# A hybrid diffusion step on one core: modulation vectors on 32-column quarters of the array, and four key heads projected before the vectors' second half

## The chip, the core and the metric

The kernel runs on one core of a Trainium2 chip. It is one launch; the metric is its device time in microseconds. Before the change three runs took 2576.31, 2579.31 and 2580.29 us, median 2579.31.

## What is computed

One layer of a hybrid backbone over 128 context tokens and 2048 latent tokens of 1024 features: modulated RMS norm, a combined projection into gated DeltaNet heads and gated spatial MLP groups, output projection, modulated norm, a squared-ReLU MLP, and a last norm. The change touches only the opening: the modulation vectors and the first projection.

```python
def modulation(cond, w_mod_l, b_mod_l):
    m = jax.nn.silu(cond) @ w_mod_l + b_mod_l
    return jnp.split(m[:, None, :], N_MOD, axis=-1)

def block(x, s0, mod, ...):
    sh1, sc1, ga1, sh2, sc2, ga2 = mod
    h = rmsnorm(x, norm_mix_l) * (1.0 + sc1) + sh1
    o, s_new = mixer(h, s0, ...)
    ...

def mixer(h, ...):
    proj = h @ w_in_l
    ...
    qkv = jax.nn.silu(centred_conv(qkv, conv_l))
```

There are two condition vectors, one for the context and one for the latent tokens (`c_ctx`, `c`), so each modulation product is a 2 x 1024 matrix times a 1024-column part of `w_mod`. All is float32.

## The kernel before

The 17 tiles of 128 tokens go through the first stage in six blocks of up to three tiles (`BLOCKS`). Features lie on partitions, as eight pieces k = 0 to 7 of 128 (`KT`). A projection is three fp32r products per k (`mm3`, L220 to L222): high part times high part, low times high, high times low; each operand is split into a high and a low part by ACT and DVE (`split_w`: ACT casts `raw` to `wH`, L191, DVE subtracts for `wL`, L192).

The opening goes as follows. `scond` (128 x 8 x 2) holds the activated condition vectors. A modulation vector is computed in halves of 512 columns: the scale `a1` and the shift `b1` of the first norm have four such halves, m0 (first half of b1), m1 (first half of a1), m2 and m3 (second halves of b1 and a1). `mod_load` fetches one as eight pieces of 256 KB. `mod_columns` makes eight fp32 products that add into two rows of one PSUM bank (L335, stationary `scond[:, k, :]`, 2 columns), copies them to SBUF on ACT (L337), and turns the 2 x 512 row into columns by four transposes (L340); DVE adds the bias and forms the scale (L343, L347).

The first half of the vectors serves k = 0 to 3, the second half k = 4 to 7. `column(k)` in `prep_block` makes the modulated features of one k for the first block: three transposes of the normalised token tiles (L482), two evictions on ACT with scale and shift (`full`, L484), then cast and subtraction on DVE (`kH`, L487, and `kL`, L488). `feature_tile` projects one head of one kind (`gi` 0 queries, 1 keys, 2 values); its `main` steps are the eight k. `first_half` shifts the halo columns, which POOL copies into `kH` and `kL`. `norm_rows` squares a token tile on ACT (L318), takes the root on POOL (L178) and scales on DVE (L320). The three token tiles and the 10 halo rows `xh` share three buffers, so the third tile takes the buffer of `xh` once that has been transposed (L387). `make_masks` builds masks on POOL from a DVE memset (L129, L135, L137) and DVE combines them (L141). Beside the block's projections run the alpha/beta projection (`ab_block`, L609, L610) and one more modulation vector (`split_mod_steps`, L359, L360).

All loads and stores are issued by SyncE, in one order; eight are in flight at a time, and the next is issued when the eighth before it has landed. The order on each engine is not the program's text: the build schedules the instructions, and what stands in the built program decides. Each engine then works through its own list and waits at semaphores.

Of the kernel before, what the change touches and what calls it, by code (L numbers as in the profile page):

```python
# [8 lines left out]
F32 = mybir.dt.float32  # L9
# [5 lines left out]
ALU = mybir.AluOpType  # L15
# [47 lines left out]
def hybrid_step(  # L63
# [217 lines left out]
    with ExitStack() as ph:  # L281
# [27 lines left out]
        V.scalar_tensor_tensor(out=st_, in0=st_, scalar=1.0, in1=cvec, op0=ALU.add, op1=ALU.mult)  # L309
        V.tensor_scalar_mul(scond.rearrange("p k c -> p c k"), st_.rearrange("p (c k) -> p c k", c=2), 0.5)  # L310

        def norm_rows(dst):

            np_ = dst.shape[0]
            junk = p1.tile([P, D], BF16, tag="junk", name="junk", bufs=1)
            ss = smp.tile([P, 1], F32, tag="ss", name="ss")
            r = smp.tile([P, 1], F32, tag="r", name="r")
            A.activation(junk[:np_, :], dst, AF.Square, accum_out=ss[:np_, :])  # L318
            rsqrt_cols(r[:np_, :], ss[:np_, :], 1, 1.0 / D, EPS)
            V.tensor_scalar_mul(dst, dst, r[:np_, :])  # L320
# [7 lines left out]
            return [raw_w(w_mod[0, k * P : (k + 1) * P, c0 + half * 512 : c0 + half * 512 + 512])  # L328
                    for k in range(KT)]

        def mod_columns(raws, half, dst, bias, scaled):

            pm = pm1()
            for k in range(KT):
                T.matmul(pm[0:2, :], scond[:, k, :], raws[k], start=k == 0, stop=k == KT - 1)  # L335
            row = p1.tile([2, 512], F32, tag="mrow", name="mrow", bufs=1)
            A.copy(row, pm[0:2, :])  # L337
            pc = pm1()
            for i in range(4):
                T.transpose(pc[:, 2 * i : 2 * i + 2], row[:, i * P : (i + 1) * P], ident[0:2, 0:2])  # L340
            ks = slice(half * 4, half * 4 + 4)
            d = dst[:, :, ks]
            V.tensor_tensor(out=d, in0=pc[:, 0:8].rearrange("p (k c) -> p c k", c=2),  # L343
                            in1=bias[:, ks].unsqueeze(1).to_broadcast([P, 2, 4]), op=ALU.add)
            if scaled:
                for cd in range(2):
                    V.scalar_tensor_tensor(out=dst[:, cd, ks], in0=dst[:, cd, ks], scalar=1.0,  # L347
                                           in1=vec[:, 16 + half * 4 : 20 + half * 4], op0=ALU.add, op1=ALU.mult)
# [22 lines left out]
        load(out=vec, in_=v_columns)  # L371
        convw = vec[:, 32:68].rearrange("p (w a) -> p w a", w=3)
        m1 = mod_load(0, D)
        mod_columns(m0, 0, b1, vec[:, 0:8], False)


        xh = p1.tile([P, D], F32, tag="x", name="xh", bufs=3)[0:10, :]
# [19 lines left out]
        def load_w1(gi, ks):  # L397
            return [w1_raw(gi, k) for k in ks]
# [329 lines left out]
        blk, xs_, cols = prep_block(0)  # L728
        for st in xs_:
            st()  # L730
        m2 = mod_load(1, 0)
        m3 = mod_load(1, D)
        wr = load_w1(1, range(4))
        mod_columns(m1, 0, a1, vec[:, 8:16], True)
        W1[1] += [split_w(r) for r in wr]
        first_half(0)
        abr = p1.tile([P, KT, 16], F32, tag="abr", name="abr", bufs=1)
        load(out=abr, in_=w_ab)
        wk = load_w1(1, range(4, KT))
        wr = load_w1(0, range(KT))  # L740
        us = [feature_tile(blk, 0, 1, h) for h in range(3)]
        for k in range(4):
            cols[k]()
            for u in us:
                u["main"][k]()
        mod_columns(m2, 1, b1, vec[:, 0:8], False)
        mod_columns(m3, 1, a1, vec[:, 8:16], True)
        W1[1] += [split_w(r) for r in wk]
        first_half(1)
        for k in range(4, KT):  # L750
# [9 lines left out]
        for bi in range(len(BLOCKS)):  # L760
            nxt = prep_block(bi + 1) if bi + 1 < len(BLOCKS) else None
            if bi == 0:
                order = [(1, 0), (1, 1), (1, 2), (0, 0), (0, 1), (1, 3), (0, 2), (0, 3)]
            else:
                order = [(gi, h) for gi in (1, 0) for h in range(4)]
            order = order + [(2, h) for h in range(4)]
            at = {e: n for n, e in enumerate(order)}
            tile_of = {}
            for n, (gi, h) in enumerate(order):
                u = us[n] if bi == 0 and n < 3 else feature_tile(blk, bi, gi, h)  # L770
                tile_of[gi, h] = u
                main = u["main"][4:] if bi == 0 and n < 3 else u["main"]
                if bi == 0 and n < 2:
                    side += wq[4 * n : 4 * n + 4]
                if bi == 0 and 2 <= n <= 5:
# [1334 lines left out]
```

## Time and profile before

| what | us |
|---|---|
| median of three runs | 2579.31 |
| span of the profiled execution, first to last instruction | 2574.7 |
| TensorE busy in it | 2542.1 (99%) |
| VectorE, ScalarE, GpSimd busy | 1781.9, 1192.5, 313.9 |
| first projection (first L220) begins | 41.30 |

The page gives the profiled execution's span; no separate time for that execution is listed, and the span lies 4.6 us below the median of the runs. Reading the rows: PE is TensorE's matmul stream, PEld its weight loads, DVE VectorE, ACT ScalarE, POOL GpSimd, SPq the issuing of transfers by SyncE. A row of the timeline has the start in us, the length, the engine, the line, the operation, what it writes and reads, its shape and count, and in brackets the idle time ahead of it with what ended it. An fp32 product shows as two passes, so eight products read x16. A row of a stretch has the busy time and number of instructions of PE, PEld, DVE, ACT and POOL, then the granted TensorE clock (1.00 is full), the busy share of the transfer engines and GB/s.

### The profile page before, as it was taken

How to read it: one execution, taken by the hardware profiler on the slowest of the kernel's cores; microseconds unless marked ns; L12 is line 12 of the kernel's file. 1: busy time of each engine (PE TensorE's matmuls, PEld its weight loads, DVE VectorE, ACT ScalarE, POOL GpSimd, SP SyncE). 2: the span in 40 equal slices, each digit the busy share in tenths (PEclk: the TensorE clock that was granted, in tenths of full speed). 3: DMA queues.
4: the chain of work that ended last, by engine and by line, in shares of the span. 5: the costliest groups of instructions: out<-in, count | busy, mean ns of one | idle time of the engine just before them, and what ended most of it. 6: DMA issues, size and time to landing. Idle time of an engine off the chain costs nothing.

```text
span 2574.7 us, 43713 instructions
## 1 busy us (share of the span) xinstructions
PE 2542.1 (99%) x15296; PEld 2134.4 (83%) x15296; DVE 1781.9 (69%) x3524; ACT 1192.5 (46%) x2758; POOL 313.9 (12%) x512
## 2 busy tenths in 40 slices
PE   8999999999999999999999999999999999999998
PEld 4999999788888778888888888888888888888887
DVE  5777746666667788885587887677674445675874
ACT  4755555554545556763355553333243333243441
POOL 3112112222222233331000000000000000000000
PEclk9999999999999999999999999999999999999999
DMA  8966637755555758896778798445599878786773
GB/s 293 297 221 208 197 118 231 235 165 168 165 168 177 229 185 261 280 311 209 268 219 252 214 292 284 140 144 155 177 298 310 279 261 301 238 258 212 232 251 107
DMA packets 533859, 579.77 MB, mean 225 GB/s; under 512 B 35500, under 2 KB 366684, under 8 KB 530054
## 3 DMA queue, kind: packets, MB, share of 16 engines
q1 hardware_dynamic: 533638, 576.98, 70.5%
q8 instruction: 120, 1.97, 0.3%
q14 instruction: 101, 0.83, 0.1%
HBM read 397.62 MB, written 179.22 MB: 224 GB/s over the span
## 4 chain that ended last, share of the span: by engine, by line
PE 55%; DVE 1%; issue 1%; DMA 0%; ACT 0%; POOL 0%; SPq 0%; DVEq 0%; POOLq 0%; ACTq 0%
PE f L220 17%; PE f L221 17%; PE f L222 17%; PE pj L220 1%; PE pj L222 1%; PE pj L221 1%; PE f L856 0%; PE pd L992 0%; PE pd L1096 0%; PE pd L1097 0%; DMA gr<-g_d 0%; PE pm L1418 0%; DMA x<-in_x_sample_dram 0%; PE pd L1060 0%; PE f L270 0%
## 5 line engine op out<-in xcount | busy, mean ns | idle before, releaser
L220 PE MATMUL f<-hop,zH 128*128 128x512 f32 x960 | 373.2, 389 | 0.0
L222 PE MATMUL f<-hop,zL 128*128 128x512 f32 x960 | 373.1, 389 | 0.0
L221 PE MATMUL f<-hop,zH 128*128 128x512 f32 x960 | 373.1, 389 | 0.0
L220 PE MATMUL f<-hop,wH 128*128 128x512 f32 x896 | 351.5, 393 | 0.0
L221 PE MATMUL f<-hop,wH 128*128 128x512 f32 x896 | 348.9, 390 | 0.0
L222 PE MATMUL f<-hop,wL 128*128 128x512 f32 x896 | 344.3, 390 | 0.0
L1604 ACT CAST zH<-zraw 128x512 fp32r<-128x512 f32 x240 | 146.5, 620 | 296.0 <-DMA zraw<-s_d 92.7
L1598 DVE TENSOR_TENSOR zL<-zraw,zH 128x512 fp32r<-128x512 f32 x240 | 162.1, 687 | 72.7 <-ACT zH L1604 61.6
L220 PEld LDWEIGHTS f<-hop,zH 128*128 128x128 f32 x960 | 180.3, 188 | 37.3
L222 PEld LDWEIGHTS f<-hop,zL 128*128 128x128 f32 x960 | 180.2, 188 | 37.3
L221 PEld LDWEIGHTS f<-hop,zH 128*128 128x128 f32 x960 | 180.2, 188 | 37.3
L222 PEld LDWEIGHTS f<-hop,wL 128*128 128x128 f32 x896 | 168.2, 188 | 35.6
L220 PEld LDWEIGHTS f<-hop,wH 128*128 128x128 f32 x896 | 168.5, 188 | 34.1 <-issue 0.9
L221 PEld LDWEIGHTS f<-hop,wH 128*128 128x128 f32 x896 | 168.6, 188 | 32.2
L222 PE MATMUL pj<-kH,wL 128*128 128x386 f32 (+2 forms) x568 | 190.6, 335 | 0.0
L220 PE MATMUL pj<-kH,wH 128*128 128x386 f32 (+2 forms) x568 | 189.1, 336 | 0.3 <-DVE kH L487 0.3
L221 PE MATMUL pj<-kL,wH 128*128 128x386 f32 (+2 forms) x568 | 189.3, 333 | 0.0
L178 POOL TENSOR_TENSOR r<-rsq,nhalf 128x1 f32<-128x1 f32 (+1 forms) x38 | 22.3, 587 | 1352.4 <-DVE rsq L177 1352.4
L1751 ACT CAST wH<-s 128x512 fp32r<-128x512 f32 x96 | 58.9, 620 | 172.8 <-DVE s L1598 157.3
L537 DVE SCALAR_TENSOR_TENSOR cv<-pj,vec,cv 128x384 f32<-128x384 f32 (+2 forms) x164 | 87.1, 538 | 58.4 <-ACT cv L534 57.0
L220 PEld LDWEIGHTS pj<-kH,wH 128*128 128x128 f32 x568 | 107.1, 189 | 4.9 <-issue 4.4
L221 PEld LDWEIGHTS pj<-kL,wH 128*128 128x128 f32 x568 | 107.4, 189 | 0.6
(408 smaller groups left out, 5729.3 us busy)
## 6 DMA issues: line engine op xcount, KB each, us to landing
zraw<-z_d SPq DMA_DIRECT2D x212, 256.0 KB
raw<-in_w_ff_dram SPq DMA_DIRECT2D x128, 256.0 KB
hop<-hop_d SPq DMA_DIRECT2D x28, 1024.0 KB
z_d<-c SPq DMA_DIRECT2D x96, 256.0 KB
zraw<-s_d SPq DMA_DIRECT2D x96, 256.0 KB
raw<-in_w_mod_dram SPq DMA_DIRECT2D x80, 256.0 KB
r<-in_w_ff_dram SPq DMA_DIRECT2D x80, 256.0 KB
s_d<-s SPq DMA_DIRECT2D x64, 256.0 KB
```

The source lines that it names most:

```text
L178: G.tensor_tensor(out=out, in0=t[:np_, :n], in1=nhalf[:np_, :n], op=ALU.pow)
L220: T.matmul(ps, lh, rh, start=first and i == 0, stop=False, skip_group_check=more)
L221: T.matmul(ps, lh, rl, start=False, stop=False, skip_group_check=more)
L222: T.matmul(ps, ll, rh, start=False, stop=last and i == n - 1, skip_group_check=more)
L537: V.scalar_tensor_tensor(out=cv[:, o : o + m], in0=ps[:, s + sh : s + sh + m], scalar=convw[:, w, j : j + 1], in1=cv[:, o : o + m], op0=AL ...
L1598: V.tensor_tensor(out=out, in0=a, in1=b, op=op)
L1604: A.copy(h, src)
L1751: A.copy(h, s2)
```

## The change

`scond` is laid out again as `sc32`, 32 columns per k of which two are filled and 30 are zero. `mod_products` replaces the loop of L335: product k goes to the 32 columns of the array (and the 32 PSUM partitions) at 32 * (k % 4), so four partial sums of two products each form in the four quarters. `mod_columns` copies all 128 rows and, in place of the four transposes, multiplies by `sel`, a 128 x 2 matrix with ones that picks and adds the four quarters. The first four key weight pieces are loaded ahead of m2 and m3. Four key heads (before: three) are projected over k = 0 to 3, and between these steps the products of m2 and m3 are placed, four at a time; `in_row` fixes their order on TensorE. The list of heads of block 0 has the fourth key head ahead of the first query head.

```diff
+        sc32 = p1.tile([P, KT, 32], F32, tag="sc32", name="sc32", bufs=1)
+        V.memset(sc32, 0.0)
+        V.tensor_copy(sc32[:, :, 0:2], scond)
+        sel = smp.tile([P, 2], F32, tag="sel", name="sel", bufs=1)
+        V.tensor_copy(sel, ident[:, 0:2])
+        for j in range(1, 4):
+            V.tensor_tensor(out=sel, in0=sel, in1=ident[:, 32 * j : 32 * j + 2], op=ALU.add)
+
+        row_end = []
+
+        def in_row(fn):
+
+            start = len(tc.nc.cur_bb.bb.instructions)
+            fn()
+            made = [x for x in tc.nc.cur_bb.bb.instructions[start:] if x.engine == mybir.EngineType.PE]
+            for x in made:
+                if row_end:
+                    tc.add_manual_dep(x, row_end[-1].name, mybir.DependencyInfo(
+                        mybir.DependencyClass.NoSync, mybir.DependencyReason.DATA), reason="order")
+            row_end.append(made[-1])
...
-        def mod_columns(raws, half, dst, bias, scaled):
+        def mod_products(raws):
 
             pm = pm1()
-            for k in range(KT):
-                T.matmul(pm[0:2, :], scond[:, k, :], raws[k], start=k == 0, stop=k == KT - 1)
-            row = p1.tile([2, 512], F32, tag="mrow", name="mrow", bufs=1)
-            A.copy(row, pm[0:2, :])
+
+            def part(k0, k1):
+                for k in range(k0, k1):
+                    j = 32 * (k % 4)
+                    T.matmul(pm[j : j + 32, :], sc32[:, k, :], raws[k], start=k < 4, stop=k >= 4)
+
+            return pm, part
+
+        def mod_columns(pm, half, dst, bias, scaled):
+
+            row = p1.tile([P, 512], F32, tag="mrow", name="mrow", bufs=1)
+            A.copy(row, pm)
             pc = pm1()
             for i in range(4):
-                T.transpose(pc[:, 2 * i : 2 * i + 2], row[:, i * P : (i + 1) * P], ident[0:2, 0:2])
+                T.matmul(pc[:, 2 * i : 2 * i + 2], row[:, i * P : (i + 1) * P], sel, start=True, stop=True)
...
-        mod_columns(m0, 0, b1, vec[:, 0:8], False)
+        pm, part = mod_products(m0)
+        part(0, KT)
+        mod_columns(pm, 0, b1, vec[:, 0:8], False)
...
+        wr = load_w1(1, range(4))
         m2 = mod_load(1, 0)
         m3 = mod_load(1, D)
-        wr = load_w1(1, range(4))
-        mod_columns(m1, 0, a1, vec[:, 8:16], True)
+        pm, part = mod_products(m1)
+        part(0, KT)
+        mod_columns(pm, 0, a1, vec[:, 8:16], True)
...
-        us = [feature_tile(blk, 0, 1, h) for h in range(3)]
+        us = [feature_tile(blk, 0, 1, h) for h in range(4)]
         for k in range(4):
             cols[k]()
-            for u in us:
-                u["main"][k]()
-        mod_columns(m2, 1, b1, vec[:, 0:8], False)
-        mod_columns(m3, 1, a1, vec[:, 8:16], True)
+            in_row(lambda: [u["main"][k]() for u in us])
+            if k % 2 == 0:
+                pm, part = mod_products((m2, m3)[k // 2])
+            in_row(lambda: part(k % 2 * 4, k % 2 * 4 + 4))
+            if k == 1:
+                mod_columns(pm, 1, b1, vec[:, 0:8], False)
+            elif k == 3:
+                mod_columns(pm, 1, a1, vec[:, 8:16], True)
...
-                order = [(1, 0), (1, 1), (1, 2), (0, 0), (0, 1), (1, 3), (0, 2), (0, 3)]
+                order = [(1, 0), (1, 1), (1, 2), (1, 3), (0, 0), (0, 1), (0, 2), (0, 3)]
...
-                u = us[n] if bi == 0 and n < 3 else feature_tile(blk, bi, gi, h)
+                u = us[n] if bi == 0 and n < 4 else feature_tile(blk, bi, gi, h)
                 tile_of[gi, h] = u
-                main = u["main"][4:] if bi == 0 and n < 3 else u["main"]
+                main = u["main"][4:] if bi == 0 and n < 4 else u["main"]
```

The lines of the changed kernel stand 24 to 37 further down: L359 is now the quarter products, L369 the products with `sel`, L388 and L389 the split-modulation products, L513 the transposes of token tiles, L640 and L641 the alpha/beta projection.

How the change moves instructions, at three places. First SyncE, near the start: loads of w_mod and w_in pieces (`raw`), token tiles (`x`) and halo rows (`xh`). Before:

```order
L380 DMA xh<-in_x_sample_dram 2x1024 x5
L392 DMA x<-in_x_prompt_dram 128x1024
L392 DMA x<-in_x_sample_dram 128x1024
L184 DMA raw<-in_w_mod_dram 128x512 x16
L184 DMA raw<-in_w_in_dram 128x512 x2
L392 DMA x<-in_x_sample_dram 128x1024
L184 DMA raw<-in_w_in_dram 128x512 x2
L738 DMA abr<-in_w_ab_dram 128x128
```

and now:

```order
L411 DMA xh<-in_x_sample_dram 2x1024 x5
L423 DMA x<-in_x_prompt_dram 128x1024
L423 DMA x<-in_x_sample_dram 128x1024
L184 DMA raw<-in_w_in_dram 128x512 x4
L184 DMA raw<-in_w_mod_dram 128x512 x7
L423 DMA x<-in_x_sample_dram 128x1024
L184 DMA raw<-in_w_mod_dram 128x512 x9
L771 DMA abr<-in_w_ab_dram 128x128
```

The four key pieces moved ahead of all of m2 and m3, and the third token tile from behind 18 pieces to behind 11.

Second, TensorE from the first product to the first projections (`pj` and `pt` are PSUM banks, `pm` those of the vectors). Before:

```order
L335 MATMUL pm<-raw,scond 2x512 x8
L340 MATMUL pm<-ident,mrow 128x2 x4
L335 MATMUL pm<-raw,scond 2x512 x8
L387 MATMUL pt<-ident,xh 128x10 x8
L482 MATMUL pt<-ident,x 128x128 x2
L340 MATMUL pm<-ident,mrow 128x2 x4
L335 MATMUL pm<-raw,scond 2x512 x8
L340 MATMUL pm<-ident,mrow 128x2 x4
L335 MATMUL pm<-raw,scond 2x512 x8
L482 MATMUL pt<-ident,x 128x128
L340 MATMUL pm<-ident,mrow 128x2 x4
L359 MATMUL pm<-wH,abW 128x512
```

and now:

```order
L359 MATMUL pm<-raw,sc_248 32x512 x8
L369 MATMUL pm<-sel,mrow 128x2 x4
L359 MATMUL pm<-raw,sc_248 32x512 x8
L369 MATMUL pm<-sel,mrow 128x2 x4
L418 MATMUL pt<-ident,xh 128x10 x8
L513 MATMUL pt<-ident,x 128x128 x3
L220 MATMUL pj<-kH,wH 128x388 x2
L220 MATMUL pt<-kH,wH 128x388
L220 MATMUL pj<-kH,wH 128x388
L513 MATMUL pt<-ident,x 128x128 x6
```

The products of m2 and m3 are gone from the place ahead of the first projections; ahead of these stand only m0, m1, the halo rows and the three token tiles.

Third, TensorE where the last vector m3 ends, in the changed kernel (`sc_248` is sc32):

```order
L220 MATMUL pj<-kH,wH 128x388
L221 MATMUL pj<-kL,wH 128x388
L222 MATMUL pj<-kH,wL 128x388
L359 MATMUL pm<-raw,sc_248 32x512 x4
L369 MATMUL pm<-sel,mrow 128x2 x4
L388 MATMUL pm<-wH,abW 128x512
L389 MATMUL pm<-wL,abW 128x512
L388 MATMUL pm<-wH,abW 128x512
L640 MATMUL pm<-kH,abW 128x388
L641 MATMUL pm<-kL,abW 128x388
```

The last four quarter products follow the fourth head's projection of k = 3, and the products with `sel` follow them directly; then come the split-modulation products and the alpha/beta projection, which stood ahead of and among the first projections before. On DVE, the memset of the masks, the mask combinations and nine weight splits now stand ahead of the last bias addition; the columns of k = 4 to 7 follow it. From a place 248 us into the profile of before, the lists of all engines are the same again.

## The prediction

> **What bounds the kernel now.** I read the page first (busy time of each engine), then the busy time in stretches, then the timeline of the first 42 us, engine by engine.
>
> ```profile
> span 2574.7 us, 43713 instructions
> PE 2542.1 (99%) x15296; PEld 2134.4 (83%) x15296; DVE 1781.9 (69%) x3524; ACT 1192.5 (46%) x2758; POOL 313.9 (12%) x512
> ...
> 50.00:60.00 10.00, 10.00 (x60) 9.96 (x59) 9.96 (x28) 6.80 (x15) 5.34 (x10) 1.00 0.55 176
> ```
>
> TensorE is the bound: 2542 of 2574.7 us. Behind the first 41 us it is filled almost without a hole, so a change in the opening counts by one thing: how much TensorE work is still to be done, with its waits, once the projections have begun. In the row of 50 to 60 us it makes 60 projections in 10 us and is never idle.
>
> ```profile
> 4.42 9.17 PE L335 MATMUL pm<-raw,scond 128*2 128x512 f32 x16 [4.42 <-DMA raw<-in_w_mod_dram]
> 14.65 7.03 PE L335 MATMUL pm<-raw,scond 128*2 128x512 f32 x16
> ...
> 23.49 0.33 PE L482 MATMUL pt<-ident,x 128*128 128x128 f32 x1 [0.96 <-DVE x L320]
> ...
> 39.13 0.33 PE L482 MATMUL pt<-ident,x 128*128 128x128 f32 x1
> 39.92 0.41 PE L340 MATMUL pm<-ident,mrow 2*128 2x2 f32 x4 [0.46 <-ACT mrow L337]
> 40.25 0.50 PE L359 MATMUL pm<-wH,abW 128*128 128x512 f32 x1
> 40.59 0.40 PE L360 MATMUL pm<-wL,abW 128*128 128x512 f32 x1
> 41.30 0.59 PE L220 MATMUL pj<-kH,wH 128*128 128x388 f32 x2 [0.32 <-DVE kH L487]
> ```
>
> A modulation vector costs TensorE 7.03 us, the first of the four 9.17: 8 products in two passes each, 16 passes of 0.43 us. The last one ends where the transpose of 39.13 begins; the first projection starts at 41.30. So before the change TensorE's own vectors set the start, not the loads.
>
> **Part 1: when the projections start now.** The new order puts them behind the first-half vectors only, and behind the third token tile (the x load that is issued last).
>
> ```profile
> 14.34 0.36 SPq L392 DMA_DIRECT2D x<-in_x_prompt_dram  x1
> ...
> 15.87 10.74 SPq L184 DMA_DIRECT2D raw<-in_w_mod_dram  x16
> ...
> 28.39 0.33 SPq L392 DMA_DIRECT2D x<-in_x_sample_dram  x1
> ```
>
> ```profile
> 18.06 1.06 ACT L318 ACTIVATE junk<-x 128x1024 bf16<-128x1024 f32 x1
> ...
> 20.68 1.06 ACT L318 ACTIVATE junk<-x 128x1024 bf16<-128x1024 f32 x1 [1.47 <-DMA x<-in_x_sample_dram]
> ...
> 34.27 1.06 ACT L318 ACTIVATE junk<-x 128x1024 bf16<-128x1024 f32 x1 [0.64 <-DMA x<-in_x_sample_dram]
> ...
> 39.29 0.57 ACT L337 COPY mrow<-pm 2x512 f32<-2x512 f32 x1 [2.23 <-PE pm L335]
> 39.77 0.90 ACT L484 ACTIVATE full<-pt,b,a 128x128 f32<-128x128 f32 x2
> ```
>
> SyncE issues one 256 KB piece per 10.74 / 16 = 0.67 us, at the pace at which older ones land. Before, 18 pieces stood ahead of the third x; now 11 do (4 key pieces, 7 of w_mod). 7 x 0.67 = 4.7 us sooner: issue at 23.7. It landed 34.27 - 28.39 = 5.9 us after its issue, with as many pieces in flight ahead of it as now: 29.6. From landing to its transpose the second tile took 23.49 - 20.68 = 2.8 us: 32.4. From that transpose to the first projection it took 41.30 - 39.13 = 2.17 us, of which 0.3 went to ACT's copy of the vector row, which no longer stands there: 1.9. First projection at 34.3, a **lead of 7.0 us**. The first-half vectors are not late for it: before, with all passes one by one, the second was through at 14.65 + 7.03 = 21.7. Nor is the buffer: the third x takes that of xh, whose transposes come right behind those vectors. The new small DVE instructions (a memset, a copy, the four of sel; about 0.2 us each) lie in the wait for the first piece, which ended at 4.42, and have over 10 us to spare.
>
> **Part 2: what TensorE must now do inside that lead.**
>
> ```profile
> 701.08 1.05 PE L992 MATMUL pd<-vn,kt 128*128 128x128 f32 x8
> 702.06 0.44 PE L1212 MATMUL pd<-Y,AH 64*64 64x64 f16 x8
> ```
>
> ```profile
> 704.90 0.34 PE L1224 MATMUL pd<-R,X 64*64 64x64 f16 x5
> 705.06 0.21 PE L1228 MATMUL pd<-X,R 64*64 64x64 f16 x1
> 705.08 0.19 PE L1224 MATMUL pd<-R,X 64*64 64x64 f16 x1
> 705.11 0.19 PE L1228 MATMUL pd<-X,R 64*64 64x64 f16 x1
> 705.12 0.19 PE L1224 MATMUL pd<-R,X 64*64 64x64 f16 x1
> 705.14 0.19 PE L1228 MATMUL pd<-X,R 64*64 64x64 f16 x1
> ```
>
> (a) The 16 products of the second-half vectors, four groups of four, one product per column quarter. No row shows 32-column quarters side by side. The nearest are L1224 and L1228, 64-column pieces on the left and right half of the columns: each line starts one every 0.03 us (705.08, 705.12 and 705.06, 705.11, 705.14), two in the time of one. The program has all eight L1224 ahead of the L1228, so here a later product overtook three that waited for their own columns. I take quarters to do the same: two passes, 0.86 us, and 0.1 for four starts: 4 x 0.95 = 3.8 us. Ends: 3.4, and 13.7 if all 32 passes run one by one.
>
> (b) Turning the row into columns was four 2-row transposes (0.41 us); now it is four fp32 products with 128 x 128 weights. L992 has eight such passes in 0.98 us; with only 2 columns moving it can be less. 0.8 per vector, two vectors: 1.6 us (0.8 to 2.0).
>
> (c) The first split-modulation products (L359, L360: 40.25 to 40.9) stood ahead of the start and now stand behind it: 0.6.
>
> (d) A new wait. The second vector's four turning products come directly behind its last group, and need ACT's row copy: 39.92 - 39.2 = 0.7 us. Queued behind them on TensorE are the products of L388 and L640, which the columns of k = 4 wait behind as well. The m2 wait is covered by 12 projections and six transposes. 0.7 (0.5 to 0.8).
>
> (e) The array's speed.
>
> ```profile
> 4.00:9.00 5.00, 4.58 (x6) 0.76 (x7) 0.00 (x0) 0.00 (x0) 4.33 (x37) 1.00 0.98 338
> ```
>
> ```profile
> 8.64 0.13 PEld L335 LDWEIGHTS pm<-raw,scond 128*2 128x2 f32 x1 [0.72 <-issue]
> 9.13 0.09 PEld L335 LDWEIGHTS pm<-raw,scond 128*2 128x2 f32 x1 [0.37 <-issue]
> 9.56 0.09 PEld L335 LDWEIGHTS pm<-raw,scond 128*2 128x2 f32 x1 [0.34 <-issue]
> ```
>
> Wait and load make one pass time: 0.72 + 0.13 = 0.85 us up to 8.64, 0.43 from 9.13 on. So the first 4.7 us of work (4.42 to 9.13) went at half speed, though the granted clock of that stretch reads 1.00. Before, the vectors kept TensorE busy from then on. Now it stands still from about 23.8 (the second tile's transpose) to 32.4. If that slows it again, 4.7 us of work lose up to 2.3; some of it falls into waits for columns. I take 1.5, nearer to the full price, since the rows show it (0 to 2.3). The Trainium skill ("TensorE: Matmul & The Clock Gate", Part 1) says that the array falls to half rate after an idle window of about 3.4 us and needs as long a busy one to come back; its busy window would make (e) an estimated 1.7 and the sum 0.2 higher. The opening of this trace agrees with the rule; no wait of 3.4 us elsewhere tests it.
>
> (f) Eight changes between quarters and the whole array. Before L1212 a change costs about 0.1 us (the eight L992 at their pitch of 0.11 are through issuing at 701.96); around the old vectors (39.13, right at the end of L335) nothing. 0.4 (0 to 0.8).
>
> (g) Second-half columns. DVE has the new a1 behind weight splits and behind the masks that POOL makes. Its costs between 36 and 62 us, by kind:
>
> ```profile
> L192 DVE TENSOR_TENSOR wL<-raw,wH 128x512 fp32r<-128x512 f32 x15 | 10.7, 726 | 0.0
> L488 DVE TENSOR_TENSOR kL<-full,kH 128x256 fp32r<-128x256 f32 x8 | 3.5, 438 | 0.0
> ...
> L488 DVE TENSOR_TENSOR kL<-full,kH 128x128 fp32r<-128x128 f32 x8 | 2.5, 312 | 0.0
> L487 DVE CAST kH<-full 128x256 fp32r<-128x256 f32 x8 | 2.5, 310 | 0.0
> ```
>
> ```profile
> 48.36 0.98 POOL L135 TENSOR_SCALAR_AFFINE_SELECT sg<-one 128x128 f16<-128x128 f16 x1 [3.76 <-DVE one L129]
> ...
> 52.72 2.63 POOL L137 TENSOR_SCALAR_AFFINE_SELECT bd<-bd 128x128 f16<-128x128 f16 x5
> ```
>
> A column is four such instructions, (3.5 + 2.5 + 2.5) / 8 and 0.3 for the fourth, about 1.4 us; a split is 0.7. The memset that lets POOL begin now stands behind four columns and five splits, 9 us after the first column at about 33.6: 42.7. POOL's chain took 55.3 - 48.4 = 7.0 us, so DVE is through the masks at about 50. TensorE by then: 34.3, 48 projections at 0.17 (60 in 10 us, above) 8.2, 15 transposes 1.5, (a), (d), (e) and (b) 7.6: it ends its turning at 51.6. The masks are just not late, but the slack is thin; from there the columns of k = 4 need DVE, ACT and DVE again, covered by the L388 and L640 products and six transposes, some 3 us. I take 0.5 (0 to 2).
>
> The three key heads became four: the same products, taken earlier, with the fourth head's twelve; no cost. The sum: 3.8 + 1.6 + 0.6 + 0.7 + 1.5 + 0.4 + 0.5 = 9.1, against 7.0: **+2.1 us**.
>
> ```profile
> PE pm L359 <- ACT wH L191: 0.6, 2, 0.5
> PE pj L609 <- DVE cv L537: 0.5, 1, 0.5
> ```
>
> ```profile
> 92.88 0.62 ACT L191 CAST wH<-raw 128x512 fp32r<-128x512 f32 x1 [2.49 <-DMA raw<-in_w_mod_dram]
> ```
>
> These are TensorE's waits between 41 and 250 us that are over 0.4. Behind the first stands a load that ACT waited for: a TensorE that comes 2 us later finds it there. That returns 0.4, at most 1.4 with the second and a third of 0.3. From 248 us on all engines run the same order, so the shift stays: **+1.7 us**. The profiled span would be 2576.4; it lies 4.6 below the median of 2579.31, and I carry the shift to the median: **2581.0**. With the unknowns at their ends, quarters side by side, the forecast runs from -3.1 (debits 5.3, returned 1.4) to +5.3 (debits 12.3, returned none).
>
> **Rivals.** 0.2% of 2579.31 is 5.2 us, about what a measurement can tell from no change: faster is below 2574.1, slower above 2584.5.
>
> A. The quarters overtake nothing. Each product has two passes on its own quarter; if products begin strictly in their order, a quarter starts its first pass only beside the second pass of the one before. Five pass times, 2.15 us, a group instead of 0.95: +4.8, to 2585.8. Against it: L1228 starts ahead of L1224 pieces that stand before it. For it: those are one-pass f16 products on halves. The Trainium skill ("TensorE: Matmul & The Clock Gate", Part 3) has matmuls start and end in strict program order, which would give this time; the rows of L1224 and L1228 speak against that. Chance 0.13.
>
> B. On the other side, the change doesn't do what it says: fp32 quarters run one after another, 32 passes of 0.43 us. Group cost 3.43, that is +9.9 over the forecast: 2590.9. It decides from 1.8 us a group on, where 1.7 + 4 x 0.88 passes 5.2. For it: four fp32 streams at once are in no row. Chance 0.12.
>
> C. The third x lands sooner: the first one took 18.06 - 14.34 = 3.7 us from issue or less. Then the lead is 9.2; with (e), (f), (g) hidden and (b) at 0.8, the debits are 5.9, and with 1.4 returned 4.7 us are gained: 2574.6, at the border of faster. Chance 0.07.
>
> **How the numbers follow.** Forecast 0.68 (its own range 2576.2 to 2584.6), A 0.13, B 0.12, C 0.07. Faster: half of C and a little of the forecast's lower end that I can't price, 0.08. Slower: B, two thirds of A and 0.05 of the forecast's upper end: 0.25. Same: 0.67. The range takes in C and leaves out B: 2574 to 2588.
>
> **What would show it.** First L220 at 34.3 (later: the x load or its normalisation). Four products of the new L359 starting within 0.2 us, the next transpose about 1.0 behind the first: the forecast; 2.2 is A, 3.4 is B. LDWEIGHTS waits or projections at double pitch from 34 to 38: (e). A wait of L369 on ACT's copy of 0.7: (d). A wait of the fifth column's L220 on DVE or POOL: (g). The L549 transpose that stands at 247.8 us before would stand at about 249.5. It would be wrong if the loads of the second-half w_mod pieces, now behind the key pieces, came later than 36 us, or if TensorE found new waits between 60 and 250 us.

## The result, and the profile after the change

| kernel | median, us | lowest to highest | runs |
|---|---|---|---|
| before | 2578.51 | 2576.2 to 2580.29 | 5 |
| changed | 2596.0 | 2593.53 to 2599.52 | 5 |

The ratio is 1.0072 (95% interval 1.0061 to 1.0082): 17.5 us slower. The forecast was 2581.0, with a range to 2588. The profiled execution has a span of 2591.8 us, 17.1 more than before.

Where along the span those 17 us lie is read from the same instruction in both timelines. First the timeline of TensorE before the change, at three places:

```profile
247.80 0.49 PE L549 MATMUL pt<-ident,x 128*128 128x128 f32 x3
...
1200.01 0.38 PE L1096 MATMUL pd<-S,qT 128*128 128x128 f32 x2
...
2560.22 0.39 PE L221 MATMUL f<-hop,zH 128*128 128x512 f32 x1
```

and the same three instructions in the changed kernel:

```profile
250.87 0.49 PE L580 MATMUL pt<-ident,x 128*128 128x128 f32 x3
...
1202.98 0.38 PE L1133 MATMUL pd<-S,qT 128*128 128x128 f32 x2
...
2577.21 0.40 PE L221 MATMUL f<-hop,zH 128*128 128x512 f32 x1
```

The shift is 3.07 us at 248, 2.98 at 1200 and 16.99 at the end. So 3 us come from the opening, where the change was made, and **14 us come behind 1200 us, in code that the change doesn't touch**. The costliest groups of the page show what got slower there; `hop` are the seven tiles per pass that move through the array in the closing stages, `w` and `z` the weights. Before:

```profile
L220 PE MATMUL f<-hop,zH 128*128 128x512 f32 x960 | 373.2, 389 | 0.0
L222 PE MATMUL f<-hop,zL 128*128 128x512 f32 x960 | 373.1, 389 | 0.0
L221 PE MATMUL f<-hop,zH 128*128 128x512 f32 x960 | 373.1, 389 | 0.0
```

and in the changed kernel:

```profile
L221 PE MATMUL f<-hop,zH 128*128 128x512 f32 x960 | 376.6, 393 | 0.0
L220 PE MATMUL f<-hop,zH 128*128 128x512 f32 x960 | 376.5, 393 | 0.0
L222 PE MATMUL f<-hop,zL 128*128 128x512 f32 x960 | 375.9, 392 | 0.0
```

Same count, no idle time ahead of them, 3 to 4 ns more each. The mean hides two kinds. The timeline of TensorE in the changed kernel around 2000 us:

```profile
1999.76 0.40 PE L221 MATMUL f<-hop,zH 128*128 128x512 f32 x1
...
2003.73 0.39 PE L220 MATMUL f<-hop,zH 128*128 128x512 f32 x1
...
2005.12 0.39 PE L220 MATMUL f<-hop,zH 128*128 128x512 f32 x1
...
2008.97 0.39 PE L222 MATMUL f<-hop,zL 128*128 128x512 f32 x1
```

From 1999.76 to 2003.73 there are 17 steps from product to product: 233.5 ns each. From 2005.12 to 2008.97 there are 17 as well: 226.5 ns. The kernel before goes at 226.7 ns in this stage. The slow stretch works on other hop tiles than the fast one (between 2003.73 and 2005.12 the next tile has begun, and its first six products still take 231.7 ns each), and that is the place to ask what distinguishes two tiles.

The opening, in the timeline of TensorE in the changed kernel:

```profile
34.09 0.99 PE L220 MATMUL pj<-kH,wH 128*128 128x388 f32 x2 [1.43 <-DVE kH L518]
...
35.52 1.48 PE L513 MATMUL pt<-ident,x 128*128 128x128 f32 x6
...
38.41 1.06 PE L359 MATMUL pm<-raw,sc 128*32 128x512 f32 x8
39.41 0.55 PE L513 MATMUL pt<-ident,x 128*128 128x128 f32 x3
```

```profile
51.87 1.05 PE L369 MATMUL pm<-sel,mrow 128*128 128x2 f32 x8 [0.78 <-ACT mrow L366]
...
54.97 0.52 PE L640 MATMUL pm<-kH,abW 128*128 128x388 f32 x1
55.29 0.53 PE L641 MATMUL pm<-kL,abW 128*128 128x388 f32 x1
...
56.69 1.24 PE L513 MATMUL pt<-ident,x 128*128 128x128 f32 x6
57.68 0.60 PE L220 MATMUL pj<-kH,wH 128*128 128x388 f32 x2
...
68.93 0.41 PE L220 MATMUL pj<-kH,wH 128*128 128x388 f32 x1 [1.15 <-DVE cv L568]
```

and the busy times of the ten us around the second of these places (PE, PEld, DVE, ACT, POOL, then granted clock, DMA share, GB/s):

```profile
50.00:60.00 10.00, 9.16 (x48) 7.55 (x48) 7.90 (x29) 5.86 (x13) 2.81 (x10) 0.83 0.78 243
```

The first projection stands at 34.09 (forecast 34.3) and a group of four quarter products takes 39.41 - 38.41 = 1.00 us (forecast 0.95). At 35.5 and again at 55 to 57 everything takes about twice its time: 0.32 us from one 388-column product to the next instead of 0.17; the granted clock of the second place reads 0.83.

### The profile page after: what moved, and what is told of

Same layout as the page of the kernel before. It is cut to its first block, busy times and chain, and to the rows that moved or that the text cites. A ratio compares the mean times of both kernels' runs of the same rounds, so it can differ in the third digit from the quotient of the medians.

```text
span 2591.8 us, 43761 instructions
## 1 busy us (share of the span) xinstructions
PE 2545.9 (98%) x15312; PEld 2137.3 (82%) x15312; DVE 1781.1 (69%) x3530; ACT 1192.5 (46%) x2758; POOL 320.6 (12%) x512
## 4 chain that ended last, share of the span: by engine, by line
PE 60%; DVE 3%; DMA 1%; issue 1%; SPq 0%; ACT 0%; POOL 0%; DVEq 0%; POOLq 0%; ACTq 0%
PE f L220 17%; PE f L221 17%; PE f L222 17%; PE pj L220 2%; PE pj L222 2%; PE pj L221 2%; PE pd L1029 1%; PE pd L1133 1%; PE pd L1134 1%; DMA ga<-gate_d 0%; PE pd L1097 0%; PE pm L1455 0%; PE f L893 0%; PE pd L1224 0%; DVE x L886 0%
```

## The experiments

**Two theories** for the 14 us. M: the addresses. `sel` is a tile of 8 bytes in the pool `smp`, which is kept to the end. The built program lays it out with 32 bytes, so every later tile on that side of SBUF (weights, `raw`, five of the seven hop tiles) lies 32 bytes further up. The two other hop tiles (the "far" ones) are laid out from the other end and stay at 196480 and 212864. A listing of instructions in order shows none of this. Against M: something in the new order or pace of the opening lasts on to the end, and addresses do nothing.

**First four runs**, which move addresses alone. An unused 8-byte tile in the kernel before (`b_pad32`); all seven hop tiles moved by 32 bytes against the weights, in the kernel before (`b_hop32`); `sel` widened to 64 bytes in the changed kernel (`a_sel64`); the far hop tiles moved along by 32 bytes in the changed kernel (`a_hop32`).

```diff
 b_pad32
+        V.memset(smp.tile([P, 2], F32, tag="pad", name="pad", bufs=1), 0.0)
 a_sel64
-        sel = smp.tile([P, 2], F32, tag="sel", name="sel", bufs=1)
+        sel = smp.tile([P, 16], F32, tag="sel", name="sel", bufs=1)[:, 0:2]
 a_hop32 (b_hop32: the same, and such a tile ahead of the five in hops["B"])
+        if n and not padded:
+            padded.append(hops["A"].tile([P, 8], F32, tag="pad", name="pad", bufs=1))
+            V.memset(padded[0], 0.0)
```

> The kernel before, with one tile of 8 bytes a row more in the small pool (and its memset in the first us), nothing else. M: the same mixture of offsets as in the changed kernel, hop products with the two hop tiles at the far end of SBUF at 233 to 234 ns, 14 us in all: 2592.5 us. P: no change, 2578.5.

> The kernel before, with all seven hop tiles moved by 32 bytes and the weights left on multiples of 64: every hop product has unequal offsets. M: all 5568 at 233 to 234 ns, that is 2880 x 6.7 ns + 1792 x 5.1 ns + 896 x 5.6 ns = 33 us: 2612 us, all of it behind 1150 us. S gives about as much here. If it is only the two far tiles that are slow with shifted weights (a bank or port of that end of SBUF): no change or a few us.

> The changed kernel, with the tile of sel made 64 bytes a row instead of 8 (32 as laid out), so that every tile behind it in SBUF starts 32 bytes further and on a multiple of 64 again, as before the change; the order of all engines is that of the changed kernel. Theory M (the late loss is a slower pace of products whose moving tile and weights lie at different offsets modulo 64 bytes): the products with hop keep 227 to 229 ns as before, the shift stays at the 3.1 us that the opening leaves at 248 us, 2581.6 us beside 2578.5. Rival P (the late loss comes from the changed opening, by the phase of loads and engines, not from addresses): 2596 as the changed kernel. Between (2585 to 2592): both.

> The changed kernel, with the two hop tiles that still lie on multiples of 64 moved down by 32 bytes, so that every hop tile and every weight tile lies 32 bytes past one. M: equal offsets again, 227 to 229 ns, 2581.6 us. Rival S (a start 32 bytes past a multiple of 64 costs by itself): all products slow, 233 to 234 ns, 2612 us, no better than the changed kernel's 2596 in any case.

| run | median, us | ratio to before (95%) |
|---|---|---|
| b_pad32 | 2590.98 | 1.0053 (1.0040 to 1.0067) |
| b_hop32 | 2611.05 | 1.0130 (1.0115 to 1.0146) |
| a_sel64 | 2597.77 | 1.0078 (1.0065 to 1.0091) |
| a_hop32 | 2596.27 | 1.0077 (1.0063 to 1.0091) |

An unused tile of 8 bytes makes the kernel before 13.9 us slower than its 2577.05 in the same comparison; its shift is 0.44 us at 248, 0.12 at 1200 and 12.8 at 2500. Moving all hop tiles costs 34.0, of which 33 was forecast. The page of b_hop32 has the same groups slower still:

```profile
L220 PE MATMUL f<-hop,zH 128*128 128x512 f32 x960 | 379.2, 395 | 0.0
```

So addresses it is. But a_sel64 and a_hop32, which M at first expected to be healed, were not: a multiple of 64 bytes is not enough. I therefore took from the built programs where each hop tile and its weights start, and from the traces the mean time from one product's start to the next. The three runs of `a_sel128`, `a_sel256` and `a_p1sel` were made to find the multiple that counts: `sel` of 128 and of 256 bytes in `smp`, and `sel` in the pool `p1` of the first stage, which leaves every later address as before.

```diff
 a_sel128 (a_sel256: [P, 64])
+        sel = smp.tile([P, 32], F32, tag="sel", name="sel", bufs=1)[:, 0:2]
 a_p1sel
+        sel = p1.tile([P, 32], F32, tag="sel", name="sel", bufs=1)[:, 0:2]
```

> The changed kernel with 128 bytes a row for sel, so that the two far hop tiles and the weights differ by 128 bytes modulo 512. If 128 is the modulus of M2: as a_p1sel, 2580 to 2582 us. If it is 256 or more: 2596 us, with the two far hop tiles at 233 to 234 ns and the other five at 227 to 229.

> The changed kernel with 256 bytes a row for sel: the two far hop tiles and the weights differ by 256 modulo 512. If the modulus is 256: far tiles at 226 to 229 ns a product like the others, a span of about 2582. If it is 512: far tiles at 233 to 234 ns and a span of 2593 to 2596.

> The changed kernel with sel in the pool of the first stage, whose space is given back, so that weights and hop tiles lie at the very addresses that they had before the change; the order of all engines is that of the changed kernel. Theory M2 (a product with hop takes 227 to 229 ns when moving tile and weights differ by a multiple of some power of two of at least 128 bytes, 233 to 234 when they differ by 32 or 64): all hop products at 227 to 229, the shift stays at the 3 to 4.7 us that the openings left at 248 us: 2580 to 2582 us. Rival P (the late loss comes from the changed opening): 2596.

Medians: a_sel128 2597.18, a_sel256 2586.4 (one run), a_p1sel 2584.28 (ratio 1.0023, 1.0013 to 1.0032). The last two lie 2 to 4 us above the 2582 that was expected at most, although their hop products are as fast as before; what is left is taken up below. The page of a_p1sel has the groups of hop as before to the digit:

```profile
L220 PE MATMUL f<-hop,zH 128*128 128x512 f32 x960 | 373.2, 389 | 0.0
```

All nine kernels together, worked out as said; "start" is the hop tile's start less the weights', modulo 256 bytes, and a pair of times is ns per product in the w and the z stage:

```
kernel     far tiles: start, ns        near tiles: start, ns
before       0    228.6  226.7            0    228.7  226.7
a_p1sel      0    228.6  226.7            0    228.7  226.7
a_sel256     0    228.6  226.7            0    228.7  226.8
after      224    234.0  233.4            0    228.7  227.8
b_pad32    224    234.0  233.4            0    228.7  227.6
a_sel64    192    234.4  233.3            0    228.8  228.4
a_hop32    192    234.3  233.3            0    228.8  227.5
a_sel128   128    233.5  232.9            0    228.8  227.3
b_hop32    224    233.9  233.3           32    234.5  233.4
```

In all nine kernels: where the two operands start a multiple of 256 bytes apart, a product takes 226.7 to 228.8 ns; at each other distance tried (32, 128, 192 and 224) it takes 232.9 to 234.5. The place of a tile by itself is not what counts: near tiles and weights that are both shifted by 32 bytes (`after`) stay fast. In the changed kernel that is 768 x 5.4 + 1224 x 6.7 ns = 12.3 us on the far tiles' products; 1655 near products of the z stage at 1.1 ns more add 1.8. Together 14.1, where the shift grew by 14.0. The near ones' loss sits right behind each change from a far tile to a near one: in the z stage of the changed kernel the first five products there take 230.1, 235.6, 228.4, 232.2 and 230.8 ns on average and the later ones 226.8 or less, which makes 1.4 of the 1.8 us. Why five is open.

**The opening.** What remains is a_p1sel's 6.1 us (3.4 to 8.3 by its interval). Its profile and that of the changed kernel run the same order, yet the shift at 248 us is 8.69 and 3.07. TensorE's waits between 33 and 250 us in a_p1sel, longest sum first:

```profile
PE pm L270 <- DVE acc L256: 2.5, 1, 2.5
PE pj L220 <- DVE kH L518: 1.4, 1, 1.4
PE pj L220 <- DVE cv L568: 1.4, 2, 1.2
PE pj L220 <- DVE rsq L177: 1.0, 1, 1.0
PE pm L369 <- ACT mrow L366: 0.8, 1, 0.8
PE pj L220 <- POOL kH L508: 0.5, 1, 0.5
```

and the first of them in its timeline, with the busy times of that stretch (PE, PEld, DVE, ACT, POOL, clock, share, GB/s):

```profile
130.97 0.49 PE L580 MATMUL pt<-ident,x 128*128 128x128 f32 x3
134.01 3.05 PE L270 MATMUL pm<-acc,pick 128*2 128x512 f32 x4 [2.55 <-DVE acc L256]
136.99 0.69 PE L220 MATMUL pj<-kH,wH 128*128 128x386 f32 x1
```

```profile
120.00:140.00 20.00, 17.19 (x84) 13.69 (x83) 18.42 (x35) 6.83 (x14) 0.29 (x1) 0.91 0.85 274
```

Behind a wait of 2.55 us the four L270 take 3 us instead of 2, and the granted clock of the stretch falls to 0.91. In the changed kernel the same wait is 1.0 and the clock stays at 1.00:

```profile
129.83 1.02 PE L270 MATMUL pm<-acc,pick 128*2 128x512 f32 x2 [1.04 <-DVE acc L256]
```

```profile
120.00:140.00 20.00, 18.80 (x105) 16.41 (x104) 19.93 (x38) 7.29 (x22) 0.43 (x1) 1.00 0.79 244
```

Up to 69 us the two profiles stand level (the wait on `cv` ends at 68.85 and 68.93). Of the 5.6 us between their shifts, 1.3 have come by 80 us in a_p1sel (most of it the wait on `rsq`), 2.5 by 123, 4.2 at the end of the long wait and 5.4 by 138, behind the slow stretch. The waits on `kH`, on ACT and on POOL were in the forecast; those on `acc`, `cv` and `rsq`, 4.9 us together, were not. Seven runs try to remove them, all from a_p1sel on: three key heads and the old order of heads, as before the change (`a_three`); the second group of m3 ahead of the projections of k = 3 (`a_m3`); the masks at the start (`a_mask`); an own buffer for `xh`, so that the third token tile loads right behind the second (`a_x`); that with block 0's halo copies for k >= 4 on ACT in place of POOL (`a_x_halo`); and two sums, `a_m3hk` (a_m3, masks, halo) and `a_all` (that and `xh`).

```diff
 a_three
-        us = [feature_tile(blk, 0, 1, h) for h in range(4)]
+        us = [feature_tile(blk, 0, 1, h) for h in range(3)]
 a_m3
+            if k == 3:
+                in_row(lambda: part(4, 8))
+                mod_columns(pm, 1, a1, vec[:, 8:16], True)
 a_mask: make_masks() moved ahead of sc32
 a_x
-        xh = p1.tile([P, D], F32, tag="x", name="xh", bufs=3)[0:10, :]
+        xh = p1.tile([P, D], F32, tag="xh", name="xh", bufs=1)[0:10, :]
 a_x_halo, besides
+                    halo = A.copy if bi == 0 and k >= 4 else G.tensor_copy
+                    halo(kH[:, col : col + 1], f32(halH)[:, k, j : j + 1])
+                    halo(kL[:, col : col + 1], f32(halL)[:, k, j : j + 1])
```

> As a_p1sel (2584.3 us), with three key heads over k = 0 to 3 as before the change, and the old order of heads. If the fourth head's bank is what the wait at 67 us (1.2 us on DVE's convolution) and the later waits on DVE come from: 2 to 4 us less, 2580.5 to 2582. Rival: with less work between the vectors' groups the columns of k = 4 to 7 come later still, no change or 1 to 2 us more: 2584 to 2586.

> As a_p1sel, with the second group of the last vector's products placed ahead of the four heads' projections of k = 3 instead of behind them, so that twelve projections stand between it and the products with sel. Theory of the opening: ACT's copy of the row is then hidden (0.8 us), and without the idle time and the two-column products in one stretch the array does not fall to half speed at 54 us (8 products of 0.32 instead of 0.175 us and six transposes, 1.7 us): 2.0 to 2.5 us less than a_p1sel, 2578 to 2579.5. Rival: the half speed comes back at another place or the columns of k = 4 wait for DVE, and no more than the 0.8 us is gained.

> As a_p1sel, with make_masks called at the start of the first stage, so that POOL's 7 us and DVE's combinations lie in the first 20 us, where both wait. If DVE's and POOL's load between 40 and 60 us is what the later waits come from (in a_p1sel 0.5 us on POOL at 57 and some 5 us on DVE's convolution, accumulation and root between 66 and 150 us): 2 to 4 us less than a_p1sel: 2580 to 2582. Rival: these waits come from the new order of the heads and stay: 2583.5 to 2585.

> As a_p1sel, with a buffer of its own for the halo rows, so that the third token tile is loaded right behind the second instead of behind 11 pieces (issue at 15.9 instead of 23.4 us). Theory of the opening (the third tile's landing sets the first projection): landing at 21.5, first L220 at 27 instead of 34.1, and 5 to 7 us less than a_p1sel: 2574 to 2577. Rival: the second halves of the vectors or the later key pieces come too late for the earlier start, and the gain is given back by 60 us: 2580 to 2582.

> As a_x (third token tile loaded early), with the halo copies of k = 4 to 7 of the first block on ACT instead of POOL. Theory H (POOL's small copies crawl while DVE is busy without a gap: four took 7.6 us in a_x, from 51.1 to 58.7 us, and that wait also dropped the array to half speed until 63): the wait of 7.6 us at 50.8 falls below 1 us and the half speed behind it goes, 9 us less than a_x: 2578 to 2582. Rival: something else on DVE is late for k = 4 just as long, and less than 4 us is gained: 2585 or more.

> As a_m3, with the masks at the start and the halo copies of k = 4 to 7 on ACT: the wait of 1.3 us on POOL at 55 us goes as well, and what a_mask gains later: 2578.5 to 2580.5 (a_m3: 2583.0). Rival as for a_mask: 2581.5 to 2583.

> All of it: addresses of before, third token tile early, last vector's products one step earlier, masks at the start, halo copies on ACT. First projection at 27 us as in a_x, no wait over 1 us until 66 us: a shift of -3 to -1 us at 248 us: 2574 to 2577.5 us, faster than before by 1 to 4 us. Rival: the earlier start is given back at waits on DVE between 60 and 150 us, since DVE has the same work to do in less time: 2578 to 2581.

| run | median, us | ratio to before (95%) |
|---|---|---|
| a_p1sel | 2584.28 | 1.0023 (1.0013 to 1.0032) |
| a_three | 2582.31 | 1.0014 (1.0005 to 1.0023) |
| a_m3 | 2582.98 | 1.0020 (1.0011 to 1.0029) |
| a_mask | 2585.64 | 1.0031 (1.0020 to 1.0042) |
| a_x | 2588.81 | 1.0041 (1.0028 to 1.0053) |
| a_x_halo | 2582.42 | 1.0020 (1.0011 to 1.0029) |
| a_m3hk | 2584.93 | 1.0033 (1.0020 to 1.0046) |
| a_all | 2581.18 | 1.0015 (1.0006 to 1.0024) |

None of the eight medians lies inside the range that its theory gave. Most of the intervals overlap: a_x is slower than a_three and a_all by more than they allow, while a_x and a_x_halo just touch. a_three gives back 2.0 us, which its interval does not tell from nothing. In its profile the wait on `rsq` is gone and those of L270 sink to 0.8 in all, but the wait on `cv` stands there with three heads as it did with four:

```profile
PE pj L220 <- DVE cv L568: 1.2, 1, 1.2
```

So the fourth head is not what that wait comes from, and whether it cost anything stays open. In a_m3 the wait for ACT's row copy is gone and the one on POOL has grown from 0.5 to 1.3. a_mask tells little of the masks: its edit also changed SyncE's order, the third token tile went from behind 11 pieces to behind 15, was issued at 26.05 instead of 23.43, and the first projection came at 36.97 instead of 34.14 (a_m3hk: 37.19). The wait on POOL stayed at 0.5.

The opening is not all of it either. In some profiles the shift grows once more between 248 and 1200 us, from 2.95 to 8.03 in a_three and from 5.72 to 9.90 in a_sel256, each with a wait of 3 us or more on `P` (L1213) near 531 us; in the profile of the changed kernel it stays (3.07 and 2.98). What sets off those waits is open, so a median of this table holds more than the opening.

a_x has its first projection at 27.36, 6.8 us sooner than a_p1sel, and loses all of it and more. TensorE and POOL in a_x:

```profile
58.43 1.01 PE L220 MATMUL pj<-kH,wH 128*128 128x388 f32 x2 [7.61 <-POOL kH L508]
```

```profile
51.10 7.63 POOL L508 CAST kH<-halH 128x1 fp32r<-128x1 f32 x4 [1.24 <-DVE halH L441]
58.67 0.54 POOL L509 CAST kL<-halL 128x1 fp32r<-128x1 f32 x4
```

```profile
50.60:58.30 7.70, 0.22 (x3) 0.00 (x0) 7.70 (x31) 3.91 (x9) 7.20 (x1) 0.66 0.63 182
```

Four one-column copies take 7.63 us, and it is the first of them alone that takes 7.27, ending at 58.37; the other three take 0.18 each, and so do the four behind them. Through all of that first copy VectorE is busy without a gap (7.70 of 7.70). The Trainium skill ("SBUF — State Buffer", Who interferes with whom) has VectorE and GpSimd share a port pair by an exclusive lock, so that the loser waits through the other's whole instruction. These rows agree that POOL waits, but the copy stood through some 25 VectorE instructions in a row (51.1 to 58.3 us), not one. With these copies on ACT, a_x_halo is 6.4 us faster than a_x by the medians (9 expected), but then meets a wait of 5.3 us on VectorE's convolution `cv`. In a_all that wait can be followed back. TensorE, then ACT:

```profile
65.24 0.66 PE L220 MATMUL pj<-kH,wH 128*128 128x388 f32 x1 [5.28 <-DVE cv L570]
```

```profile
61.51 1.06 ACT L467 ACTIVATE junk<-x 128x1024 bf16<-128x1024 f32 x1 [6.47 <-DMA x<-in_x_sample_dram]
62.57 1.34 ACT L567 ACTIVATE cv<-pj,vec 128x128 f32<-128x128 f32 x4
```

ACT stands at the square of the next block's token tile for 6.47 us, until its load lands; the convolution, which would give TensorE back a PSUM bank, is queued behind it. Two runs move the steps of the next block's token tiles back, by two heads (`a_all2`) and by one with three key heads (`a_all3`). A third fills TensorE's empty stretch ahead of the first projection with five products that nothing reads (`a_warm`, on a_all3), to keep it from half speed.

```diff
 a_all2
-                    side += nxt[1][n : n + 1]
+                    side += nxt[1][n : n + 1] if bi else nxt[1][n - 2 : n - 1] if n > 1 else []
 a_all3
+                    side += nxt[1][n - 1 : n] if bi == 0 and n else nxt[1][n : n + 1] if bi else []
 a_warm, besides
+        def warm(n):
+            in_row(lambda: [T.matmul(spare[:, 0:256], ident, flat, start=True, stop=True) for _ in range(n)])
```

> As a_all (2581.2 us), with the next block's token tiles handled two heads later, so that on ACT the first convolution stands ahead of their squares. In a_all TensorE waited 5.3 us at 60 us for that and ran at half speed until 68: both gone, 5 to 7 us less: 2574.5 to 2576.5, faster than before. Rival: the next block's columns then come too late, and the gain is lost before 150 us: 2580 or more.

> Three key heads, the third token tile early, m3 one step earlier, masks at the start, halo copies on ACT, the next block's token tiles one head later, addresses of before. If both causes hold: 2573 to 2576. If three heads leave too little work ahead of the second-half columns: 2577 to 2580.

> a_all3 (2576.8 us) with five fp32 products of 256 columns, which nothing reads, placed on TensorE in the gaps between 20 and 26.7 us (one behind the halo transposes, one behind each of the first two token transposes, two behind the third). If idle time is what keeps the array at half speed: the first projections (26.7 to 30.7 us in a_all3) run at 0.17 us apart instead of 0.32, the first four groups of k = 0 end 1.5 to 2.4 us sooner, 2574.5 to 2575.5 us if it is kept. Rival: the gaps are too short to bring full speed back, or the fillers delay the transposes: 2576 to 2578.

| run | median, us | ratio to before (95%) |
|---|---|---|
| a_all2 | 2583.42 | 1.0016 (1.0007 to 1.0025) |
| a_all3 | 2576.76 | 0.9996 (0.9987 to 1.0005) |
| a_warm | 2576.55 | 0.9995 (0.9986 to 1.0004) |

a_all2 missed: the waits moved on (3.9 us on `cv`, 2.2 on `ev`). a_all3 is the first without a loss; its shift at the place of 247.80 is -1.08 us. a_warm does to TensorE what it was made for. The stretch of 27 to 31 us in a_all3, then in a_warm:

```profile
27.00:31.00 4.00, 4.00 (x15) 3.64 (x14) 3.01 (x10) 2.00 (x5) 2.80 (x14) 0.53 1.05 387
```

```profile
27.00:31.00 4.00, 4.00 (x25) 2.80 (x24) 3.44 (x11) 2.84 (x7) 3.93 (x18) 0.84 1.05 386
```

The granted clock there is 0.84 in place of 0.53 and TensorE passes 25 instructions in place of 15 (two of the 25 are fillers, eight the first quarter products). Its first projection comes 0.84 us later and the first group of quarters still 0.68 sooner (30.34 for 31.02). The total shows nothing of it; in its profile the shift is -0.63 us at 248 and 4.90 at 1200, once more by waits behind the opening. Neither of the two best versions can be told from the kernel before.

## Why the prediction was wrong, point by point

- **The step that failed: "From 248 us on all engines run the same order, so the shift stays".** The order is the same; the pace is not. A small tile in a long-lived pool moved the weights against the far hop tiles, and 14.0 of the 17.1 us between the two profiles come from that. b_pad32, which has nothing of the change but such a tile, shows 13.9; a_p1sel and a_sel256 take it away. No rival held it: all three were about the opening. Even without addresses the shift need not stay: in a_three 5.1 us are added between 248 and 1200.
- First projection: 34.09 for 34.3. The x load was issued at 23.35 (23.7) and ACT's square of it began at 29.38 (29.6). Right.
- (a) 1.00 us a group for 0.95: right. Rivals A (2.15) and B (3.43) fall with it. Only in the first-half vectors, ahead of the first projection, did two groups in one row take 4.00 us (at 12.93). That was the loads: from the fifth product on, each weight load waits 0.48 to 0.66 us for its piece of w_mod (13.80, 14.47, 15.26, 15.88), at a granted clock of 1.00.
- (b) 0.91 us a vector for 0.8, from 51.87 to the next product at 52.78: within its bounds. (d) 0.78 for 0.7. (f) about 0.1 a change into quarters. (c) 0.77 for 0.6 (52.78 to 53.55).
- (e) The first half-speed stretch cost about 1.5 us as forecast; in a_p1sel it cost 1.0 more. A second one, 54 to 57.5 us, was not forecast: 1.7 us. It is in the profile of the changed kernel and not in that of a_p1sel, which runs the same order with the same 0.78 us wait ahead of it. The Trainium skill ("TensorE: Matmul & The Clock Gate", Part 1) has a free-running window of about 3.4 us that judges activity, so that the same program meets it at another phase from run to run. The traces agree with that: their records of the granted clock show half speed for 3.41 us or a whole multiple of it, here from 54.12 to 57.54, and in steps of 3.41 the wait of 51.09 to 51.87 and the two-column products behind it lie inside one window (50.71 to 54.12), while in a_p1sel an edge at 52.79 cuts through the wait. That the Trainium skill asks for an idle window of that length is not borne out: windows with waits of 0.78 and, at 134 us, 2.55 were enough. No run shifts the phase on purpose, so this stays argued. The prediction's 1.00 for 4 to 9 us of the kernel before is no measurement: the clock record of that trace begins at 8.77 us.
- (g) No wait in the profile of the changed kernel, 0.5 in a_p1sel: as taken. But the reason was another: POOL's halo copies stood while VectorE was busy (a_x), and with the masks moved away the wait of 0.5 stayed (a_mask).
- "The three key heads became four: no cost". Not refuted. The wait of 1.15 us on `cv` at 67.8, longer than the 0.5 of the kernel before, is there with three heads as well (a_three, 1.15 at 67.92), and the 2.0 us that a_three gives back are not clear of noise.
- "That returns 0.4": the waits on `wH` went, but `cv`, `acc` and `rsq` came, 1 to 2.5 us each. The prediction named "new waits between 60 and 250 us" as what would make it wrong and gave them no term. So the opening's +1.7 became +3.1 in one profile and 8.7 in another; in medians 3.6 (17.5 less b_pad32's 13.9) to 6.1 (a_p1sel), and the intervals of these two overlap. In the two profiles the spread comes between 69 and 138 us, from longer waits on VectorE and the slow stretch behind the longest; why the same order waits longer in one execution is open.

The change in its own place thus bought a lead of 7.2 us and paid some 11 to 13 for it (the lead plus the medians' 3.6 to 6.1); without its address effect it is still a loss (a_p1sel), and it comes to even only in a_all3 (and a_warm on top of it), with three heads, an earlier third tile, m3 one step earlier, the masks at the start, the halo copies off POOL and the next block's steps later. Which of these are needed was not tried one by one.

## What to carry to other kernels

When code is added ahead of a long uniform stage, compare the addresses of the two builds and not only their instruction order, and put small tiles into a pool that dies with its stage, or pad them to 256 bytes, so that later tiles move by a distance that kept the pace here. A lead at the start is worth only what every later holder of a buffer can follow: VectorE was near its limit behind the opening (19.93 of 20 us busy from 120 to 140 in the changed kernel), and a wait that was taken away often stood up again further on (`kH` on POOL in a_x, then `cv` in a_x_halo and a_all2). An estimate that ends in "the rest is unchanged" needs a look at the costliest groups' mean time, which a shift of a few ns times thousands of products turns into the whole result.

## What the runs showed of the hardware

- TensorE's pace depends on how far apart its two operands start in SBUF: 226.7 to 228.8 ns for a product at a multiple of 256 bytes, 232.9 to 234.5 at the other distances tried, for fp32r products of 512 columns. The first five products behind a change from a slow distance to a fast one are slow as well (228.4 to 235.6). What in the memory causes it was not tried.
- Four fp32 products on four 32-column quarters, eight passes, take 1.00 us (38.41 to 39.41 in the changed kernel); one after another, at the 0.43 us a pass of the kernel before, they would take an estimated 3.43.
- TensorE falls to half speed for 3.41 us or a whole multiple of it, by the clock records of these traces (the stretch that a trace's end cuts off aside). Behind the first 42 us of the 19 profiles, 16 of the 17 waits of 2.0 us or more have such a stretch in or right behind them (L270 in a_p1sel, a_m3, a_sel128 and a_all: 0.91 from 120 to 140 us); the waits of 0.7 to 1.6 at L270 have none. The one exception, 530.31 to 532.35 in a_m3, is cut by an edge of its 3.41 us steps at 531.86.
- POOL's one-column copy: 7.27 us while VectorE was busy without a gap, 0.18 for each of the seven behind it.
